# One output tile's store cut at row 50 instead of row 104, in a matmul with bias and residual

The kernel runs on one core of a Trainium2 chip. The metric is the device time of one execution in microseconds (us), lower is better. The experiments ran on three chips (7, 11 and 15), so a difference of a few tenths means something only within the same rounds.

## What the kernel computes

```python
batch, m, k, n = 16, 512, 1024, 768            # x, weight, bias, residual: float32
out = np.matmul(x, weight) + bias + residual   # float32, 16*512 rows of 768
```

The 8192 output rows are 64 tiles of 128 rows. A tile of the output is 128 partitions with one row of 3072 bytes each. Tiles are numbered 0 to 63; tile 58 is near the end.

## The kernel before

One list gives the order of all transfers. `('s', S, j0, j1)` stores tiles 16*S+j0 to 16*S+j1-1; a further number cuts that store into two pieces at that row. `'c'` stores the two column parts of the last tile.

```python
ORDER = [
 # ... loads of x, weight, bias, residual, and earlier stores left out ...
 ('s', 3, 0, 10), ('s', 3, 10, 11, 104), ('s', 3, 11, 13),
 ('s', 3, 13, 14), ('s', 3, 14, 15), ('c', 3, 15, 0), ('c', 3, 15, 1)]
OUTSIDE = 4
```

The part that issues a store. All transfers go out from one engine, SyncE, in the order of the list:

```python
                edges = [0, *cut, P]
                for p0, p1 in zip(edges, edges[1:]):
                    dma(out_d[S, p0:p1, j0:j1, n0:n0 + nl],
                        R[p0:p1, t0 % RR:t0 % RR + j1 - j0, n0:n0 + nl], rows(t0, t0 + j1 - j0, cs), [])
                    stores.append(len(prog.ops) - 1)
```

And the end of the program, which waits for every store:

```python
        for sem, value in landed[:-OUTSIDE]:
            nc.sync.wait_ge(sem, value)
    with tc.tile_critical(sync_engine=mybir.EngineType.SP):
        for sem, value in reversed(landed[-OUTSIDE:]):
            nc.sync.wait_ge(sem, value)          # L395 in the profile
```

## Time and profile before

| of the kernel before | value | from |
|---|---|---|
| time, median of the first 3 executions | 210.48 us (210.28 to 210.52) | timing |
| profiled execution | 210.92 us, span 209.1 us | timing, page |
| TensorE busy | 200.4 us, 96% | page, part 1 |
| last VectorE add ends | 204.56 us | timeline |
| last store landed | 207.74 us | semaphore updates in the trace |

Times within an execution count from the start of the profile's span. The page's part 1 gives an engine's busy time, part 2 the busy share in 40 slices, part 4 the chain that ended last. For the end of this kernel the windows view matters more, since the DMA engines still work when no compute engine does.

### The profile page before, as it was taken

What the parts mean: (1) busy time and instruction counts of PE and PEld (TensorE: products, weight loads), DVE (VectorE), ACT (ScalarE), POOL (GpSimd) and SP (SyncE); (2) the same over time, 40 slices, a digit from 0 to 9 for tenths busy, and PEclk for the clock granted to TensorE, in tenths of its full rate; (3) what the DMA queues carried; (4) which work ended last, traced back from release to release, by engine and by line L of the source; (5) the groups of instructions that cost most, each with busy time, mean ns of one, the idle gap of its engine ahead of it and who ended that gap; (6) DMA issues with size and microseconds to landing.
All of it is one profiled execution on the core that took longest, in us unless ns stands there. A gap on an engine that the chain in (4) does not pass through costs nothing.

```text
span 209.1 us, 2471 instructions
## 1 busy us (share of the span) xinstructions
PE 200.4 (96%) x1273; PEld 80.9 (39%) x794; DVE 105.3 (50%) x141; ACT 66.1 (32%) x69; POOL 115.1 (55%) x71
## 2 busy tenths in 40 slices
PE   7899999999999999999999999999999999999990
PEld 2333433443443344344434433443443344344440
DVE  1458555445545544654455454645545544554451
ACT  2444513402640372310370093320091055330000
POOL 1100029759999805998039702999108950999000
PEclk9999999999999999999999999999999999999997
DMA  6999999999989999999999999999999999998994
GB/s 222 424 429 436 432 414 471 391 449 411 495 377 486 389 410 418 442 447 407 428 450 450 411 423 479 404 423 412 424 482 423 421 415 472 451 432 366 441 360 162
DMA packets 4924, 87.20 MB, mean 417 GB/s; under 512 B 557, under 2 KB 685, under 8 KB 1841
## 3 DMA queue, kind: packets, MB, share of 16 engines
q1 hardware_dynamic: 4913, 87.05, 97.7%
q8 instruction: 8, 0.13, 0.2%
q14 instruction: 3, 0.02, 0.0%
HBM read 61.88 MB, written 25.17 MB: 416 GB/s over the span
## 4 chain that ended last, share of the span: by engine, by line
PE 91%; DMA 4%; issue 1%; DVE 1%; SPq 0%; ACT 0%
PE psum_o L249 78%; PE pt L242 13%; DMA x_tile<-in_x_dram 4%; SPq L160 0%; DVE xt L218 0%; ACT xb L218 0%; DVE ro L221 0%; SPq L395 0%; SPq L363 0%
## 5 line engine op out<-in xcount | busy, mean ns | idle before, releaser
L249 PE MATMUL psum_o<-w_sb,xt 128*128 128x256 bf16 (+1 forms) x999 | 175.3, 324 | 1.8 <-DVE xt L218 0.5
L221 POOL TENSOR_TENSOR ro<-ro,bias_sb 128x768 f32<-128x768 f32 x50 | 88.8, 1811 | 46.8 <-DMA ro<-in_residual_dram 46.8
L218 ACT CAST xb<-x_tile 128x1024 bf16<-128x1024 f32 (+1 forms) x63 | 61.3, 1023 | 117.1 <-DMA x_tile<-in_x_dram 80.1
L260 PEld LDWEIGHTS <-xt 128*128 128x128 bf16 x520 | 50.9, 98 | 102.9 <-issue 101.0
L218 DVE COPY xt<-pt 128x1024 bf16<-128x1024 bf16 x64 | 44.1, 691 | 83.6 <-PE pt L242 83.6
L221 DVE TENSOR_TENSOR ro<-psum_o,ro 128x768 f32<-128x768 f32 (+2 forms) x51 | 47.6, 934 | 6.3 <-POOL ro L221 4.3
L242 PE MATMUL pt<-ident,xb 128*128 128x128 f32 x256 | 38.3, 273 | 0.5 <-DVE xb L218 0.3
L221 POOL TENSOR_TENSOR ro<-ro 128x768 f32<-128x768 f32 x14 | 24.9, 1813 | 25.0 <-DMA ro<-in_residual_dram 25.0
L242 PEld LDWEIGHTS pt<-ident,xb 128*128 128x128 f32 x256 | 29.7, 140 | 15.5 <-issue 12.3
L221 DVE TENSOR_TENSOR ro<-psum_o,bias_sb 128x768 f32<-128x768 f32 x14 | 13.2, 948 | 0.0
L304 PE MATMUL psum_o<-warm 128*128 128x512 bf16 x18 | 6.4, 514 | 1.4 <-DVE warm_a L224 1.4
L218 DVE CAST xb<-x_tile 128x512 bf16<-128x512 f32 (+1 forms) x4 | 1.9, 492 | 6.1 <-DMA x_tile<-in_x_dram 6.1
L218 ACT CAST w_sb<-ro 128x768 bf16<-128x768 f32 x4 | 3.3, 832 | 3.7 <-DMA ro<-in_weight_dram 3.7
L218 POOL CAST w_sb<-ro 128x768 bf16<-128x768 f32 x1 | 0.8, 824 | 5.9 <-DMA ro<-in_weight_dram 5.9
L304 PEld LDWEIGHTS psum_o<-warm 128*128 128x128 bf16 x18 | 2.2, 126 | 4.6 <-issue 2.9
L218 DVE CAST w_sb<-ro 128x768 bf16<-128x768 f32 x3 | 1.7, 557 | 2.0 <-DMA ro<-in_weight_dram 2.0
L218 ACT ACT_TABLE_LOAD x1 | 1.3, 1283 | 0.9 <-SPq L363 0.9
L321 DVE STREAM_SHUFFLE bias_sb<-bias_row 128x768 f32<-128x768 f32 x1 | 1.0, 1024 | 0.0
L224 DVE MEMSET warm<- 128x256 uint32 x1 | 0.3, 272 | 1.1 <-SPq L363 1.1
L224 DVE MEMSET bias_row<- 128x768 f32 x1 | 0.7, 698 | 0.2 <-issue 0.2
L224 POOL MEMSET ident<- 128x128 f32 x1 | 0.2, 204 | 0.5 <-SPq L363 0.5
L312 POOL TENSOR_SCALAR_AFFINE_SELECT ident<-ident 128x128 f32<-128x128 f32 x1 | 0.3, 293 | 0.2 <-POOL ident L224 0.2
(7 smaller groups left out, 0.7 us busy)
## 6 DMA issues: line engine op xcount, KB each, us to landing
out_dram<-ro SPq DMA_DIRECT2D x3, 6144.0 KB, 34.4
x_tile<-in_x_dram SPq DMA_DIRECT2D x3, 5120.0 KB, 24.5
ro<-in_residual_dram SPq DMA_DIRECT2D x3, 3840.0 KB, 32.1
x_tile<-in_x_dram SPq DMA_DIRECT2D x3, 3072.0 KB, 39.8
ro<-in_residual_dram SPq DMA_DIRECT2D x3, 2304.0 KB, 18.5
x_tile<-in_x_dram SPq DMA_DIRECT2D x4, 1024.0 KB, 10.9
x_tile<-in_x_dram SPq DMA_DIRECT2D x2, 2048.0 KB, 23.4
out_dram<-ro SPq DMA_DIRECT2D x1, 3840.0 KB, 13.1
```

The costliest lines, as they stand in the source:

```text
L218: op(eng, lambda e: (e.copy if eng == "act" else e.tensor_copy)(out=dst, in_=src), rd, wr)
L221: op(eng, lambda e: e.tensor_add(out=dst, in0=a, in1=b), rd, wr)
L224: op(eng, lambda e: e.memset(dst, v), [], [wr])
L242: op("pe", lambda e, q=q: e.transpose(out=pt[:, q, :], in_=words[:, ts(q, P)], identity=ident), [("XB", t % XB_N, 2 * q // n_q), "ident"], ...
L249: return e.add_instruction(mybir.InstMatmult(name=nc.get_next_instruction_name(), ins=[e.lower_ap(rhs), e.lower_ap(lhsT, for_matmul_weight ...
L260: op("pe", lambda g: g.ldweights(lhsT), rd)
L304: op("pe", lambda e: e.matmul(PO[i][:, 0:512], lhsT=warm[:, 0:P], rhs=warm, start=True, stop=True), ["warm"], [("PO", i)])
L312: op("pool", lambda e: e.affine_select(out=ident, in_=ident, compare_op=mybir.AluOpType.not_equal, fill=1.0, base=0, pattern=[[-1, P]], ch ...
L321: op("dve", lambda e: e.stream_shuffle(out=bias_sb, in_=bias_row, mask=[0] * QUAD), ["bias_row"], ["bias"])
```

## The change

Its intent: spread tile 58 differently over the DMA engines. Neither cut gives the three highest-numbered engines any of it; the prediction counts the rows of each engine.

```diff
- ('s', 3, 10, 11, 104)
+ ('s', 3, 10, 11, 50)
```

## The prediction

> **What bounds the kernel now.** I read the page first, for the whole kernel, and then only its last ten microseconds, because the change touches one store near the end. First the heads of the page and its chain of work.
>
> ```profile
> span 209.1 us, 2471 instructions
> PE 200.4 (96%) x1273; PEld 80.9 (39%) x794; DVE 105.3 (50%) x141; ACT 66.1 (32%) x69; POOL 115.1 (55%) x71
> DMA  6999999999989999999999999999999999998994
> PE 91%; DMA 4%; issue 1%; DVE 1%; SPq 0%; ACT 0%
> ```
>
> TensorE is busy for 96% of the span and the chain that ended last is 91% TensorE: matmuls set the pace until the last output tile. The DMA row says that the 16 DMA engines are just as full all the way. So compute sets when the last data are ready, and the DMA engines, which carry a backlog, set when those data are out. The page's chain ends at the last VectorE add and says nothing of the stores after it. The windows view of the last microseconds does; its columns are the stretch, its length, busy time and count of PE, PEld, DVE, ACT and POOL, the granted clock, the DMA share and GB/s.
>
> ```profile
> 203.00:204.00 1.00, 1.00 (x10) 0.68 (x7) 0.67 (x1) 0.00 (x0) 0.00 (x0) 1.00 0.96 390
> 204.00:205.00 1.00, 0.09 (x1) 0.00 (x0) 0.44 (x2) 0.00 (x0) 0.00 (x0) 1.00 0.82 328
> 205.00:206.00 1.00, 0.00 (x0) 0.00 (x0) 0.00 (x0) 0.00 (x0) 0.00 (x0) 1.00 0.94 355
> 206.00:207.00 1.00, 0.00 (x0) 0.00 (x0) 0.00 (x0) 0.00 (x0) 0.00 (x0) 0.95 0.33 117
> 207.00:208.00 1.00, 0.00 (x0) 0.00 (x0) 0.00 (x0) 0.00 (x0) 0.00 (x0) 0.50 0.02 8
> ```
>
> TensorE and VectorE stop by 204.6 us; DMA goes on until 207.4, at 0.94 of all engines in one microsecond, then 0.33, then 0.02. A share of 0.02 of 16 engines is a third of one engine: the end is one late engine. The waits of the issuing queue from 190 us on (total, times, longest) say whom it waits for:
>
> ```profile
> SPq L160 <- DVE ro L221: 12.1, 6, 3.7
> SPq L395 <- DMA out_dram<-ro: 1.6, 3, 0.6
> ```
>
> And the DMA issues of this stretch name the stores (size of one issue, then median time from issue to landing):
>
> ```profile
> out_dram<-ro SPq DMA_DIRECT2D x2, 384.0 KB, 4.8
> out_dram<-ro SPq DMA_DIRECT2D x1, 312.0 KB
> out_dram<-ro SPq DMA_DIRECT2D x1, 256.0 KB, 3.4
> out_dram<-ro SPq DMA_DIRECT2D x1, 128.0 KB, 3.2
> out_dram<-ro SPq DMA_DIRECT2D x1, 72.0 KB
> ```
>
> The last thing that the program does is to wait on L395 for the final stores. The 312 KB and 72 KB issues are the two pieces of tile 58 (104 and 24 rows of 3 KB), the ones that the change resizes. They alone have no landing time, since fewer than 16 DMA engines report for them.
>
> **The 16 engines one by one.** The views give only the mean of the engines. But a packet of an engine that has work queued starts within 4 ns of the end of the one before it, and each engine gets a known sequence of packet sizes, so I linked the trace's packet records into 16 chains. What they show: a row of 3072 B takes 121 ns and the next starts 118 ns after it. Engines finish the store before tile 58 (tiles 48 to 57) between 198.85 and 200.96. Twelve then carry 8 + 2 rows of tile 58, one carries 8, three carry none, and all carry equal shares of the four stores behind it. Eight of the 16 (among them the three without tile 58) later stand idle for want of work, 0.33 to 0.98 us each. The eight others never idle. The last two of these are far apart: one ends at 206.89, the last at 207.41, and the last landing is at 207.74. That last engine carries 8 + 2 rows of tile 58. It is late for two reasons: a 16 KB packet of the instruction queue held it 0.93 us at 191.66, with two slow neighbours (1.63 and 1.54 against 1.14 us); and its ten rows took 1.74 us, not 1.18, three of them at 267, 412 and 222 ns.
>
> **What the Trainium skill says.** (1) "DMA: Bandwidth & Descriptors", section "Why a DMA increments its semaphore by 16 and not by 1": a transfer runs on the largest k up to 16 that divides its slowest dimension, on the lowest-numbered k engines. The trace agrees on k: 13 and 12 landings for 104 and 24 rows, 16 for all others. For the change, 50 gives 10 and 78 gives 13. (2) The same page, "Queues, rings and completion order": each engine takes its descriptors in ring order, so rows added ahead push back what comes behind on that engine. The unbroken chains agree. (3) "Runtime: NRT & Kernel Launch", section "Instruction fetch mechanics": instructions are refilled in 16 KiB blocks over DMA. The trace has eight 16 KB packets on another queue, about 24 us apart, on different engines. (4) "SBUF — State Buffer", section "Door 1: The DMA port swizzle": which of 16 ports a partition is read through follows from bits of its number; a 128-row transfer gives each engine one port. A split by 13, 12 or 10 does not keep to that, so two engines may meet at a port. The trace fits but does not prove it: between 192.7 and 199.1 next to no packet is slow, while from 199.1 to 202.7, with tile 58 in flight, some twenty take 1.5 to 6 times their usual time.
>
> **The change part by part.** Work on PE, DVE, ACT and POOL: none, the instruction order of these engines is the same. On the issuing queue: still two issues, of other sizes. They stand at 191.40 and 191.80, the second taking 1.93 us, done by 193.73; the next store waits for VectorE until 197.48, so 3.7 us of slack hide any difference. Bytes and rows: the same 128 rows. What moves is who carries them. Engines 0 to 9: 5 + 6 = 11 rows in place of 10, so +1 x 0.118 = +0.12 us. Engines 10 and 11: 6 in place of 10, so -4 x 0.118 = -0.47 us. Engine 12: 6 in place of 8, so -0.24 us. Engines 13 to 15: none, as before. Only the last engine counts. Ten of the twelve candidates get the extra row, and linking its chain back to the small bias load, which only four engines carry, puts it (less surely) among engines 0 to 3. So the plain sum is +0.12 us: its last packet moves from 207.41 to 207.53, and the 1.3 us between the last landing and the end of the span stay.
>
> **The rivals.** (a) *The slow packets move.* They cost the last engine 0.56 us here, and eight of the 13 engines that carry tile 58 had none at all. With other rows on other engines it may meet nobody: 207.41 + 0.12 - 0.56 = 206.97, and the second engine, 206.89 + 0.12 = 207.01, then sets the end, 0.40 us sooner. For it: the slow packets come exactly with the uneven splits. Against it: the new splits are uneven too, over more rows in the second piece. (b) *They get worse* on the last engine, or land on the second one: 0.12 plus about 0.4, so half a microsecond slower. (c) *The last engine is another one in runs without the profiler*: were it 10, 11 or 12, it gains 0.24 to 0.47 us, and the next engine, with its extra row, sets an end 0.40 sooner at best; were it one of 13 to 15, nothing changes. The three times before lie within 0.24 us, which speaks against a different class of engine from run to run. (d) *It is hidden anyway*: the last VectorE add ends at 204.56 and its store lands on the idle engines by 206.56. That floor is 1.18 us below the last landing, so the extra row is not hidden.
>
> **Range and chances.** Weights: the plain sum with slow packets as before, 210.48 + 0.12 = 210.60, 0.45; (a), 210.48 - 0.40 = 210.08, 0.30; (c), about 210.10, 0.15; (b), about 211.0, 0.10. The mean is 210.42. I name 210.45, between mean and plain sum, with 210.05 to 210.85 for 8 in 10. Two per cent are 4.2 us. Faster by that much is out of reach, as only 1.18 us lie above the floor; slower would take some 36 more rows on one engine, by 0.118 us a row. So within 2% has 0.98.
>
> **What would show it right or wrong.** Right: the two tile-58 issues become 150 and 234 KB; compute ends at the same 204.6; the landings of the first piece come from 10 engines, of the second from 13; on ten engines the two pieces take 11 x 0.118 = 1.30 us where no packet is slow; the last landing moves by +0.12 if the last engine keeps its slow packets. Wrong: the last engine is one that carries 6 rows or none; the slow packets stay although no engine shares anything in time with another; the end moves while the chains before it do not, which would put the cause on the issuing queue or on the final waits. A move of more than 0.6 us either way would mean that the accounting by rows misses the main thing.

## More of the kernel before

A single look at a kernel (one execution, profiled): such looks are used here only for their traces and for differences of several microseconds.

In all 13 profiled executions of this study, the time of the execution is the last landing plus 3.18 to 3.22 us. So the last landing is the figure to explain.

## The result

The changed kernel took 210.72 us (median of 4, 210.44 to 210.86) where the kernel before took 210.5 us (median of 4, 210.28 to 211.16). The ratio was 1.0004, with a 95% interval of 0.9979 to 1.0028: the same time. A ratio here is the mean time of one kernel's runs over that of the other's runs of the same rounds, so it is not quite the ratio of the medians. The predicted figure was 210.45 us; its range of 210.05 to 210.85 holds the median.

The head of the changed kernel's page (span, busy times, DMA row, chain of work by engine):

```profile
span 208.9 us, 2496 instructions
PE 202.3 (97%) x1298; PEld 81.3 (39%) x794; DVE 105.5 (50%) x141; ACT 66.1 (32%) x69; POOL 115.1 (55%) x71
DMA  6999999899999999999999999999999999999994
PE 92%; DMA 4%; DVE 1%; SPq 0%; ACT 0%; issue 0%
```

Nothing has moved in the bulk. The 25 instructions more are matmul records that the first trace lacks (x1298 against x1273), not work. Now the windows view of the end of the changed kernel, with the same columns as in the prediction:

```profile
203.00:204.00 1.00, 1.00 (x10) 0.68 (x7) 0.62 (x1) 0.00 (x0) 0.00 (x0) 1.00 0.95 387
204.00:205.00 1.00, 0.14 (x2) 0.00 (x0) 0.49 (x2) 0.00 (x0) 0.00 (x0) 1.00 0.92 370
205.00:206.00 1.00, 0.00 (x0) 0.00 (x0) 0.00 (x0) 0.00 (x0) 0.00 (x0) 1.00 1.01 385
206.00:207.00 1.00, 0.00 (x0) 0.00 (x0) 0.00 (x0) 0.00 (x0) 0.00 (x0) 1.00 0.32 112
207.00:208.00 1.00, 0.00 (x0) 0.00 (x0) 0.00 (x0) 0.00 (x0) 0.00 (x0) 1.00 0.00 0
```

Compute ends at the same 204.6 us. The DMA engines are a little fuller until 206, and the lone late engine of the last window (0.02 before) is gone: the share is 0.00. The DMA issues from 190 to 205 us show the new pieces, 234 and 150 KB, again without a landing time, and the waits of the issuing queue are as before:

```profile
out_dram<-ro SPq DMA_DIRECT2D x2, 384.0 KB, 4.4
out_dram<-ro SPq DMA_DIRECT2D x1, 256.0 KB, 3.1
out_dram<-ro SPq DMA_DIRECT2D x1, 234.0 KB
out_dram<-ro SPq DMA_DIRECT2D x1, 150.0 KB
out_dram<-ro SPq DMA_DIRECT2D x1, 128.0 KB, 2.8
```

```profile
SPq L160 <- DVE ro L221: 12.8, 6, 4.5
SPq L395 <- DMA out_dram<-ro: 1.5, 3, 0.6
```

The semaphore updates that mark a landing come from 10 and 13 engines, as the rule that the prediction cites says. Linking the packets into 16 chains as in the prediction shows what each engine did. Where no packet was slow, 11 rows took 1.31 us against 1.19 us for 10 rows before. The three engines with 6 rows took 0.71 us each, ended early (206.09 to 206.33), and one of them had carried the last instruction packet (at 193.5; so the document calls the 16 KB packets on the queue that the trace names "instruction"). The last packet of all ended at 207.01 on an engine with 11 rows, and the last store landed at 207.47, which is 0.27 us before the first profile's 207.74.

So one pair of profiles says 0.27 us faster, and the medians say 0.2 us slower. Both are inside the spread of single executions, which is what the experiments had to take apart.

### The profile page after: what moved, and what is told of

Same layout as the page of the kernel before. It is cut to its first block, busy times and chain, and to the rows that moved or that the text cites. A ratio compares the mean times of both kernels' runs of the same rounds, so it can differ in the third digit from the quotient of the medians.

```text
span 208.9 us, 2496 instructions
## 1 busy us (share of the span) xinstructions
PE 202.3 (97%) x1298; PEld 81.3 (39%) x794; DVE 105.5 (50%) x141; ACT 66.1 (32%) x69; POOL 115.1 (55%) x71
## 4 chain that ended last, share of the span: by engine, by line
PE 92%; DMA 4%; DVE 1%; SPq 0%; ACT 0%; issue 0%
PE psum_o L249 79%; PE pt L242 13%; DMA x_tile<-in_x_dram 4%; SPq L160 0%; DVE xt L218 0%; ACT xb L218 0%; DVE ro L221 0%; SPq L395 0%; SPq L363 0%
## 5 line engine op out<-in xcount | busy, mean ns | idle before, releaser
L304 PE MATMUL psum_o<-warm 128*128 128x512 bf16 x18 | 6.9, 548 | 1.4 <-DVE warm_a L224 1.4
## 6 DMA issues: line engine op xcount, KB each, us to landing
x_tile<-in_x_dram SPq DMA_DIRECT2D x3, 5120.0 KB, 24.5
```

The costliest lines, as they stand in the source:

```text
L304: op("pe", lambda e: e.matmul(PO[i][:, 0:512], lhsT=warm[:, 0:P], rhs=warm, start=True, stop=True), ["warm"], [("PO", i)])
```

## The experiments

Theory at the outset, row accounting: each row of tile 58 on an engine costs that engine 0.118 us, and the engine that ends last sets the time. Rivals: relief of one particular late engine; slow packets that come from the uneven split itself; work shared evenly whatever the cut.

### The changed kernel again, more rounds (again)

No edit.

> The changed kernel once more, in more rounds. Row accounting: the engines that end last carry 10 rows of tile 58 before and 11 after, so +0.12 us where the last one is of engines 0 to 9 and no packet is slow. Rival, relief of the engine with the last instruction packet: it carried 10 rows and now carries 6, so up to 0.40 us faster in executions where it is last. Both together: within 0.3 us of the kernel before. In the trace: ten engines with 5 + 6 rows, three with 6, three with none.

Measured: 210.43 us median of 6 (210.28 to 210.79) against 210.78 us of the kernel before (11 executions, 210.37 to 211.28); ratio 0.9983, interval 0.9967 to 1.0. Still the same time by the 2% measure. But the kernel before now fell into two groups: six executions from 210.37 to 210.78, and five from 211.00 to 211.28. None of the changed kernel's was in the upper group. In its trace, the three engines with six rows again took 0.71 us each without a slow packet on tile 58; the last engine had 11 rows. The eight 16 KB instruction packets began at another engine: those at 23.7 and 47.3 us were on engines without tile 58, and those at 144.3, 168.4 and 193.6 on the three with six rows.

### Tile 58 in one transfer (whole)

```diff
- ('s', 3, 10, 11, 104)
+ ('s', 3, 10, 11)
```

> Tile 58 in one transfer of 128 rows: 8 rows on each of 16 engines. Row accounting: the late engines carry 2 rows less than before, so -0.24 us, and the three engines that carried none now end about 0.9 us later, near 206.5 to 207, so the gain is 0 to 0.3 us. Rival that uneven splits make the packets slow: no packet of tile 58 over 1.3 times 121 ns, and 0.3 to 0.8 us faster. Rival that the three engines without tile 58 are left out for a reason (they would be last): slower by 0.2 us or more.

Measured: 210.18 us median of 6 (210.06 to 210.29); ratio to the kernel before 0.9968, interval 0.9951 to 0.9986. That is some 0.7 us less than before (0.0032 x 210.8), and 0.25 us less than the changed kernel in the same rounds, by the medians; the interval does not reach 1. The windows view of its end:

```profile
205.00:206.00 1.00, 0.00 (x0) 0.00 (x0) 0.00 (x0) 0.00 (x0) 0.00 (x0) 1.00 0.99 374
206.00:207.00 1.00, 0.00 (x0) 0.00 (x0) 0.00 (x0) 0.00 (x0) 0.00 (x0) 1.00 0.23 79
```

The share after 206 us falls from 0.33 before and 0.32 after the change to 0.23: the sixteen engines finish closer together. Between 199.0 and 202.8 us no packet took over 1.2 times its usual time ("slow" from here on); in the first profile 15 did, for 3.0 us over all engines, and with the change 22 did, for 5.0 us. Each of the 16 engines did its eight rows in 0.95 us. So the trace bears out the rival that the slow packets come with uneven splits. The time alone does not: over the lower group of the kernel before, whose mean is 210.49 us, the gain is 0.31 us, and row accounting allowed 0 to 0.3. The next run keeps the rows per engine equal, to tell the two apart. Leaving three engines out had no merit here.

### Tile 58 in two pieces of 64 rows (half)

```diff
- ('s', 3, 10, 11, 104)
+ ('s', 3, 10, 11, 64)
```

> Tile 58 in two transfers of 64 rows, 4 + 4 rows on each of 16 engines: the same rows per engine as the whole transfer. Row accounting alone: the same time as the whole transfer within 0.1 us. Rival, ports: [...]many packets of tile 58 take about twice 121 ns, and up to 8 x 0.12 = 0.9 us more on the late engines; slower than the whole transfer by 0.2 to 0.9 us.

Measured: 210.55 us median of 6 (210.19 to 210.84), 0.37 us over the whole transfer in the same rounds; ratio to before 0.9986, interval 0.9968 to 1.0004. The rows per engine are equal, so row accounting alone fails here. Eleven packets that began between 199.0 and 202.8 us were slow, all of them rows of tile 58 (161 to 280 ns); one 30 KB row that began earlier, at 197.83, took 2.28 us against 1.14. In the traced execution, the fastest of the six, most of that fell on engines with time to spare, and the last landing, 207.00, was as early as in the whole transfer (207.03). So this trace shows the slow packets but not the loss; the timings show the loss. The port explanation is tested with a larger store below.

### Tile 58 in pieces of 127 and 1 rows (one)

```diff
- ('s', 3, 10, 11, 104)
+ ('s', 3, 10, 11, 127)
```

> Tile 58 in pieces of 127 and 1 rows. By the rule for the number of engines both pieces run on one engine, the lowest. Row accounting: that engine carries 128 rows in place of 10, 118 x 0.118 = 13.9 us more, so the end comes 13 to 14 us later, about 224 us in all, while the 15 others end some 0.5 to 1.2 us sooner. Rival, work is shared out over all engines whatever the rows: no change over 0.5 us.

Measured in one look: 223.45 us, last landing 220.24. That is 13 us over the 210.4 us of the faster executions of the kernel before. The first fence is two stretches of its windows view, the second its issues:

```profile
200.00:206.00 6.00, 4.17 (x26) 1.95 (x20) 2.64 (x4) 0.00 (x0) 0.00 (x0) 1.00 0.16 63
214.00:219.00 5.00, 0.00 (x0) 0.00 (x0) 0.00 (x0) 0.00 (x0) 0.00 (x0) 0.50 0.06 26
```

```profile
out_dram<-ro SPq DMA_DIRECT2D x1, 381.0 KB
out_dram<-ro SPq DMA_DIRECT2D x1, 3.0 KB
```

A share of 0.06 for five microseconds is one engine of 16, moving 26 GB/s. Each piece reports from one engine; the long one landed at 215.38 and the single row at 215.56, as on one and the same engine. In the linked chains one engine carries all 128 rows, from 199.03 to 215.17 us, which is 0.126 us a row with the slow ones included. So the rule for the number of engines holds, and the price of a row nearly so: 118 rows more cost 13 us, where 13.9 were counted. One side effect was not foreseen: the issuing queue was held 12.5 us at the second piece, so the stores behind it went out late on all engines (next issue at 204.31, not 197.5), and the 15 other engines ended later, not sooner (their last landing is 211.86).

### The kernel before, profiled three more times (b1, b2, b3)

No edit.

> The kernel before, profiled again, as it was seen near 210.4 and near 211.2 us in the last rounds. Theory: the late state of these is an execution in which the engine with the last instruction packet, or another late one, carries 10 rows of tile 58 and meets slow packets; then the last landing stands 0.4 to 0.8 us behind the next engine's, and slow packets on that chain make it up. In the early state the last two engines end within 0.2 us. Rival: the two states differ in the time when TensorE ends (204.1 in the first profile) by as much as the end does.

> As the run before it: if the end is near 211.2 us, one engine ends far behind the next one, with slow packets of tile 58 on its chain; if near 210.4, the last two engines end within 0.2 us. Rival: the end follows the end of TensorE's work.

> As the two runs before it. Over the three, the engine that gets the last 16 KB instruction packet is not always of the same group, as the trace of the changed kernel run twice suggests (it began at another engine).

The times were 210.48, 211.22 and 210.43 us, so both groups were caught. The windows view of b2, in the upper group:

```profile
205.00:206.00 1.00, 0.00 (x0) 0.00 (x0) 0.00 (x0) 0.00 (x0) 0.00 (x0) 1.00 0.87 336
206.00:207.00 1.00, 0.00 (x0) 0.00 (x0) 0.00 (x0) 0.00 (x0) 0.00 (x0) 0.83 0.50 179
207.00:208.00 1.00, 0.00 (x0) 0.00 (x0) 0.00 (x0) 0.00 (x0) 0.00 (x0) 0.50 0.05 16
```

Most of 0.05 of 16 engines over one microsecond is one engine again, later than in the first profile. Engine by engine:

| execution | time | last add ends | last landing | the next engine's | last engine's rows of tile 58 |
|---|---|---|---|---|---|
| before, first profile | 210.92 | 204.56 | 207.74 | 207.23 | 10, in 1.75 us |
| b1 | 210.48 | 204.62 | 207.26 | 207.25 | 10, in 1.51 us |
| b2 | 211.22 | 204.79 | 208.04 | 207.34 | 10, in 1.62 us |
| b3 | 210.43 | 204.48 | 207.24 | 207.10 | 10, in 1.59 us |
| after | 210.68 | 204.61 | 207.47 | 207.12 | 11, in 1.34 us |
| again | 210.62 | 204.62 | 207.41 | 207.15 | 11, in 1.31 or 1.33 us (two chains meet) |

In b1 two engines tie; the row names the one with slow packets. Without a slow packet ten rows take 1.19 us. In the first profile, b1 and b3, the last engine is the one that carried the last 16 KB instruction packet (191.7, 193.7 and 193.6 us); in b2 it is the one with the first (23.9 us), and on it 0.43 us of slow packets (1.62 less 1.19). So in the one trace of the upper group one late engine with slow packets on tile 58 sets the end, but the slow packets make up only about half of the delay. The last engine of b2 landed 0.78 us after the engine with the same instruction packet did in b1. Of this, 0.43 us are the slow rows of tile 58.

The other 0.35 us are much older. Compute also ended later in b2 (204.79 against 204.62 and 204.48), but that cannot have held this engine back: from 34.5 us on no packet of its chain began more than 7 ns after the one before it had ended. Its chain shows where the time went. In the load of the residual for tiles 22 to 31, one 30 KB row at 77.8 us took 1.93 us, against 1.45 to 1.58 us in the first profile, b1 and b3. The engine ended this load at 80.90 us (80.54 in b1) and carried the delay to the end. Nor is it the only engine: 30 KB rows of more than 1.2 us that began between 70 and 84 us took 7.4 us more than usual over all 16 engines in b2, and 3.0 to 3.6 us more in the other three. The windows view shows this spell as a lower rate; the first line is b1, the second b2:

```profile
76.00:80.00 4.00, 4.00 (x28) 1.60 (x16) 1.60 (x3) 1.45 (x2) 0.00 (x0) 1.00 1.02 421
76.00:80.00 4.00, 4.00 (x29) 1.66 (x17) 1.56 (x2) 1.42 (x2) 0.00 (x0) 1.00 0.94 363
```

The spell stands in all 13 traces, with 2.0 to 9.3 us, long before the transfer that was changed. What causes it, and how much of the upper group it makes, is not shown: only one execution of that group was profiled.

Which engines are these? In all four traces of the kernel before, the engine with only eight rows, which must be 12, carried the second packet (47.0 to 47.1 us), and engines without tile 58 carried the third and fourth. In the first trace of the changed kernel, the third and fourth are again on engines without tile 58, and the first, second and eighth are on the three engines with six rows, 10 to 12. If the order of engines was the same in these executions, the engines of the first and the last packet are 10 and 11. The second trace of the changed kernel and that of 108 + 20 rows, below, fit the same order of eight engines, begun at its third place. This is an inference across executions. The trace does not number the engines.

### The large store in two pieces of 64 rows (big64)

```diff
- ('s', 3, 0, 10), ('s', 3, 10, 11, 104)
+ ('s', 3, 0, 10, 64), ('s', 3, 10, 11)
```

> Tile 58 whole, and the store of tiles 48 to 57 in two pieces of 64 rows: each engine has 4 + 4 rows of 30 KB, as many as in one piece, so row accounting says no change, 210.2 us within 0.3. Rival, ports: [...]many packets of 1.14 us take up to twice that while the engines are in the same half; slow packets appear from 190 us on and the end comes 0.5 to 9 us later.

Measured in one look: 219.29 us, 9 us over the whole transfer's 210.2. The windows view while the large store is on its way:

```profile
191.00:198.00 7.00, 7.00 (x48) 2.74 (x27) 3.46 (x5) 0.00 (x0) 2.99 (x2) 1.00 1.07 252
200.00:206.00 6.00, 4.07 (x26) 1.85 (x19) 2.54 (x4) 0.00 (x0) 0.00 (x0) 1.00 0.96 195
```

The DMA engines are as busy as ever and move 252, then 195 GB/s. Each engine's four rows of a piece took 7.4 to 11 us, against 4 x 1.138 = 4.55 us. The rows per engine are those of one transfer, so rows do not explain it. The page "SBUF — State Buffer" of the Trainium skill, section "Door 1: The DMA port swizzle", says that partitions 0 to 63 reach 8 of the 16 ports and gives an asymptote (the rate that large transfers tend to) of about 218 GB/s for them. The 195 GB/s here lie 11% under it and the 252 GB/s 16% over it; in that first stretch some rows still took the usual 1.138 us. So this case agrees roughly.

### The large store in two pieces over all partitions (cols)

```diff
- for p0, p1 in zip(edges, edges[1:]): dma(rows p0 to p1 of tiles j0 to j1)
+ halves = [(j0, j0 + 5), (j0 + 5, j1)] if j1 - j0 == 10 else [(j0, j1)]
+ for a, b in halves: dma(all 128 rows of tiles a to b)
```

> Tile 58 whole, the store of tiles 48 to 57 in two pieces of 128 rows and five tiles each: two transfers, as in the run with two pieces of 64 rows, but each over all 16 ports. Ports: no slow packets, 210.2 us within 0.4 (16 KB rows cost no more per byte). Rival, two transfers of one store as such cost the 9 us: near 219 us.

Measured in one look: 210.23 us. The same stretches of its windows view, to be set beside those of the run above:

```profile
191.00:198.00 7.00, 7.00 (x48) 2.74 (x27) 3.41 (x5) 0.00 (x0) 2.76 (x2) 1.00 1.00 424
200.00:206.00 6.00, 4.01 (x26) 1.85 (x19) 2.48 (x4) 0.00 (x0) 0.00 (x0) 1.00 0.92 369
```

424 GB/s, and from 192.7 us to the end one slow packet (0.97 us against 0.57, right behind an instruction packet). One difference from the run above remains: the first piece was issued by itself, earlier, at 173 us. But the engines had a backlog, and its rows began at 189.7 us, as in the run above (189.9). Two transfers as such are not the cost; the partitions that one transfer spans are.

### Pieces of 108 and 20 rows beside the changed kernel (c108, again2)

```diff
- ('s', 3, 10, 11, 104)
+ ('s', 3, 10, 11, 108)
```

> Tile 58 in pieces of 108 and 20 rows, over 12 and 10 engines: engines 0 to 9 carry 9 + 2 = 11 rows as in the changed kernel, engines 10 and 11 carry 9 in place of 6, engine 12 to 15 none. Theory, relief of engines 10 and 11 (they get the first and the last 16 KB instruction packet): those two are late again, so executions near 210.9 to 211.2 us come back and the mean is 0.1 to 0.5 us over the changed kernel's. Rival, only the extra row on engines 0 to 9 matters: the same as the changed kernel within 0.1 us, and no execution over 210.9.

> The changed kernel in the same rounds, to be compared with the pieces of 108 and 20. All executions between 210.2 and 210.9 us, none in the late state near 211.2; the kernel before shows the late state in about a third of its executions.

Measured in the same rounds: 108 + 20 gave 210.78 us (median of 6, 210.59 to 211.33), ratio to before 0.9999 (0.9982 to 1.0016). The changed kernel gave 210.96 us (median of 6, 210.60 to 211.21), ratio 1.0006 (0.9989 to 1.0023). The kernel before gave 211.05 us (median of 11, 210.47 to 211.44). The expectation of 0.1 to 0.5 us between the two splits failed: nine rows or six on engines 10 and 11 made no difference that these rounds show, and four of the six executions of the changed kernel went over 210.9 us, one to 211.21. In the traced execution of 108 + 20 the instruction packets at 24.5, 47.1 and 193.6 us were on engines without tile 58, so the engines that they make late were others that time. In the trace of the changed kernel the last add ended at 205.04 us, 0.4 us later than in the earlier ones, at the same last landing (207.42). This run was inconclusive on the relief of engines 10 and 11, and it puts a limit to it.

That trace does show the relief at work, if not in the time. It has the longest slow spell near 77 us, 9.3 us over all engines. The engine with the first instruction packet came to tile 58 at 201.57 us, later than any in the four traces of the kernel before (201.34 at most). With its six rows it ended at 207.02, next to last. Ten rows would have taken 0.48 us more (an estimate: 1.19 less 0.71) and put it 0.43 us behind the engine that was last.

All timings together, which mixes rounds and chips: of 31 executions of the kernel before, 13 took 211.0 us or more; of 16 of the changed kernel, one did. In the rounds of the first repetition the lower group of the kernel before has a mean of 210.49 us, where all six of the changed kernel have 210.48.

## Why the prediction came out as it did

**The bound: right.** Compute ends at 204.6 us in the first profiles of both kernels, and the time follows the last landing by 3.2 us in every profile.

**One row is 0.118 us: right.** 11 rows take 1.31 us and 10 take 1.19; 118 rows more on one engine cost 13 us. Three figures beside it were slightly off: the time from the last landing to the end of the span is 1.40 us, not 1.3; the weights give a mean of 210.41, not 210.42; and of the "some twenty" slow packets, only 15 took over 1.5 times their usual time.

**What each engine carries: right.** Ten and thirteen engines report, the three with six rows take 0.71 us, and the issuing queue's slack hid the new sizes.

**Which engine counts: wrong.** The step that failed is the one that "puts it (less surely) among engines 0 to 3". It rested on linking the chain through 200 us back to the bias load. The four traces before and the first one after, taken together, point to engines 10 and 11. Those lose four rows each, and in the changed kernel no engine of that group had a slow packet on tile 58 in three traces. So the plain sum of +0.12 us for the same last engine did not happen; another engine, of 0 to 9 and with its extra row, came last.

**Rival (a), the slow packets move: right in mechanism.** It gave the end of packets as 207.01, and the trace has 207.01. The agreement to the last digit is luck: the engine that ended there, known by many slightly long packets (131 to 138 ns for 121), came to tile 58 0.29 us later than the engine with that mark in the first profile (200.79 against 200.50), and the medians did not gain.

**Rival (c): its argument failed.** The three times within 0.24 us were too few. The kernel before took 211.0 us or more in 13 of 31 executions. Nothing in the prediction foresaw that a slow spell near 77 us, which differs from execution to execution, is carried to the end by engines that never idle.

**The size.** 210.45 us was the mean of opposed cases, and the measured ratios of 1.0004, 0.9983 and 1.0006 are what opposed terms leave: an extra row on ten engines, and fewer late executions. That these two terms cancel is argued from the traces; no run separates them in time, since the run with 108 + 20 rows failed to, and the slow spell near 77 us moves the times by as much. It stays open how executions choose the engine with which the instruction packets begin, and which partitions each engine reads in an uneven split. So it is also open why engines 10 and 11 met the slow packets before, and what the spell near 77 us is.

The version that beat both is the plain one, tile 58 in one transfer: 8 rows on every engine, no slow packet on tile 58, 210.18 us.

## What to carry to other kernels

When a kernel ends on DMA engines with a backlog, count the bytes of each engine, not of the transfer: the end belongs to the one engine that is last, and the mean of the engines hides it. A split by rows that does not span all 128 partitions can cost twice, once through the number of engines and once through slow packets, so try the uncut transfer first. Profile the same kernel several times before explaining a few tenths of a microsecond, because one execution may belong to a second group, and follow a late engine's chain back far enough: with a backlog, a delay from the middle of the program can still stand at its end.

## What the Trainium skill lacked or had wrong

- "DMA: Bandwidth & Descriptors", section "Why a DMA increments its semaphore by 16 and not by 1": its rule for the number of engines held in every case tried (50, 78, 104, 24, 108, 20, 64, 127, 1 and 128 rows). It does not say that an uneven split also makes packets slow: 10 to 22 slow ones in 199.0 to 202.8 us with the cuts at 50, 64, 104 and 108, none with 128 rows.
- The same page, section "Rules for kernel authors", says of two transfers to disjoint partition halves that they serialize and aren't worth it, without a figure. Here the cost was 9 us for a store of 3.8 MB whose DMA rate fell from 424 to between 195 and 252 GB/s.
- "Runtime: NRT & Kernel Launch", section "Instruction fetch mechanics", calls the cost of a refill mostly hidden. It does not count the time of the DMA engine: each of the eight 16 KB packets took 0.89 to 1.10 us of one, on another engine each time, and not on the same ones in every execution. On an engine with a backlog this time is not hidden.
- No page says that a transfer on few engines can hold the issuing queue: 12.5 us at the second piece of the cut at 127, against 1.2 to 1.9 us at the other cuts of tile 58. Why it was held is not shown.
